# Shift and scale of the first two channel tiles: column products on TensorE instead of a running sum on VectorE

## Chip, cores and metric

The kernel runs on one core of a Trainium2 chip. The metric is the device time of one execution in microseconds (us); the median of several runs counts. Names of engines: PE is TensorE (PEld its weight loads), DVE is VectorE, ACT is ScalarE, POOL is GpSimd, SP is the engine whose queue issues most of the DMAs (transfers between HBM and on-chip memory).

## What is computed

One layer of a block with four parallel groups of attention heads, on 1024 latent tokens and 256 context tokens of width 2048, all in float32. What matters here is the start: the modulation of the normalised input by a vector that is made from the conditioning vector `c`.

```python
sh_x, sc_x, gt_x = jnp.split((jax.nn.silu(c) @ w_ada[l] + b_ada[l])[:, None, :], 3, axis=-1)
h_x = rms_norm(x, norm_g[l]) * (1 + sc_x) + sh_x
px = split_cols(h_x @ w_in[l])
```

So the shift `sh_x` and the scale `sc_x`, 2048 channels each, are a vector of 2048 entries times the first 4096 columns of the matrix `w_ada` (2048 rows). The attention, the output projection and the residual follow and are not touched by the change.

## The kernel before

**Tiles of channels.** The 2048 channels are 16 tiles of 128; on chip a channel is a partition. The first half of the latent tokens (512) is modulated and projected in five chunks of channel tiles, `chunks = [(0, 2), (2, 2), (4, 4), (8, 4), (12, 4)]` (first tile, number of tiles). The text calls them the first to the fifth chunk.

**Making a chunk** (`modulate`). First `ada_cols(k0, nk, 0, ax, shx)` makes shift and scale of the chunk: it loads `w_ada` in 16 blocks of 128 rows (tag `pt`, seven buffers of 4 KB per partition; in the first two chunks one buffer holds two row blocks, so eight buffers are filled by 16 loads of 256 KB). Each row block is multiplied by its entries of silu(c), one scalar per partition, and added to a sum `acc`: the first one or two blocks by ACT (L970), the others by DVE (L972, an operation of 512 elements per partition in the first two chunks and 1024 in the later ones). In the first two chunks there are two sums, for even and odd blocks, added at the end (L975). Then the partitions of the sum are added up by PE: for each channel tile one product with `acc` as the stationary operand and one column of ones as the moving operand (L979). DVE adds the bias and forms shift and scale (L982 to L984). Second, `h_build` transposes the normalised tokens by PE (L185), applies scale and shift by ACT (L187), and splits the result into a rounded part `b` (L188, ACT) and a rest (L189, DVE).

**Using a chunk** (`start`, `wide`, `three`). The projections of the chunk are products of 128x512 (L1099 to L1101, three for each tile and weight), 84 of them for a chunk of two tiles and 168 for a chunk of four. Their weights come by `w_piece`: a load on POOL's queue (L208) into `wr`, a rounded part `wh` by ACT (L220) and a rest `wl` by DVE (L221). A sum over chunks is kept in on-chip memory (L1135 by ACT in the first chunk, L1137 by DVE in the others).

**Ahead of the first chunk.** Four tiles of 128 tokens are loaded and normalised (`load_norm`: squares by ACT L151, small operations of DVE and ACT, L154 to L161, scaling by DVE, L163). Then 48 transposes (L1168) whose result nobody reads keep PE busy; they read the fourth of these tiles. Their PSUM tile and those of L979 and L185 share two buffers (`px`).

**What sets the order.** The code of two chunks is written interleaved (the second chunk is made while the first is used, and so on), and a scheduler then orders the instructions of each engine, under priorities; loads of `w_ada` are pinned to the order of the code on SP's queue. An engine works through its instructions strictly in that order.

Of the kernel before, what the change touches and what calls it, by code (L numbers as in the profile page):

```python
# [11 lines left out]
ALU = mybir.AluOpType  # L12
# [3 lines left out]
D = 2048  # L16
# [17 lines left out]
def hybrid_block(ctx, tc, x, c, cx, c_ctx, norm_g, w_ada, b_ada, w_in, w_out,  # L34
# [3 lines left out]
    pe, act, dve, pool, sp = nc.tensor, nc.scalar, nc.vector, nc.gpsimd, nc.sync  # L38
# [16 lines left out]
    def pin(i):  # L55
        return tc.keep_in_program_order(i) if strict[0] else i
# [5 lines left out]
    def T(shape, tag, dt=F32):  # L62
        uid[0] += 1
        return sb.tile(shape, dt, name=f"{tag}_{uid[0]}", tag=tag, bufs=BUFS[tag])

    def P(pool_, tag, bufs, n=512):
        uid[0] += 1
        return pool_.tile([128, n], F32, name=f"{tag}_{uid[0]}", tag=tag, bufs=bufs)
# [13 lines left out]
    def px():  # L82
        return P(ps, "x", 2)
# [5 lines left out]
    ident = cp.tile([128, 128], F32, name="ident")  # L89
# [76 lines left out]
    ax = cp.tile([128, 16], F32, name="ax")  # L166
    shx = cp.tile([128, 16], F32, name="shx")
# [13 lines left out]
    def h_build(k, xts, hT, a, sh, bank=None):  # L181
        hi, lo, n = hT
        tp = (bank or px)()
        for i in range(n // 128):
            pe.transpose(out=tp[:, 128 * i:128 * i + 128], in_=xts[i][k // 8][:, 128 * (k % 8):128 * (k % 8) + 128], identity=ident)  # L185
        ft = tmp()
        act.activation(ft[:, :n], tp[:, :n], AF.Identity, bias=sh[:, k:k + 1], scale=a[:, k:k + 1])  # L187
        act.copy(hi(k), ft[:, :n])  # L188
        dve.tensor_tensor(lo(k), ft[:, :n], hi(k).bitcast(F32), op=ALU.subtract)  # L189
# [760 lines left out]
    def ada_cols(k0, nk, vec, a_, s_):  # L950

        w, rb = 128 * nk, 4 // nk
        src = w_ada[0, :, 0:2 * D].rearrange("r (a n) -> r a n", a=2)
        na = min(rb, 2)
        acc = T([128, na, 2, w], "pt")
        for t in range(16 // rb):
            wt = T([128, rb, 2, w], "pt")
            for i in range(rb):
                k = rb * t + i
                if i == 0 or nk > 1:  # L960
                    ni = rb if nk == 1 else 1
                    if ni == 1:
                        pin(sp.dma_start(wt[:, i], src[128 * k:128 * k + 128, :, 128 * k0:128 * k0 + w]))
                    else:
                        for j in range(2):
                            pin(sp.dma_start(wt[:, :, j], src[128 * k:128 * k + 128 * rb, j, 128 * k0:128 * k0 + w]
                                             .rearrange("(r p) n -> p r n", p=128)))
                ak = acc[:, k % na]
                if k < na:
                    act.activation(ak, wt[:, i], AF.Copy, bias=0.0, scale=sil[:, vec, k:k + 1])  # L970
                else:
                    dve.scalar_tensor_tensor(ak, wt[:, i], sil[:, vec, k:k + 1], ak, op0=ALU.mult, op1=ALU.add)  # L972
            yield 0.25 * nk * rb
        if na == 2:
            dve.tensor_tensor(acc[:, 0], acc[:, 0], acc[:, 1], op=ALU.add)  # L975
        mp = px()
        for i in range(2):
            for j in range(nk):
                pe.matmul(mp[:, 4 * i + j:4 * i + j + 1], lhsT=acc[:, 0, i, 128 * j:128 * j + 128], rhs=ones[:, 0:1],  # L979
                          start=True, stop=True)  # L980
        ks = slice(k0, k0 + nk)
        dve.tensor_tensor(s_[:, ks], mp[:, 0:nk], bshc[:, ks], op=ALU.add)  # L982
        dve.tensor_tensor(a_[:, ks], mp[:, 4:4 + nk], bscc[:, ks], op=ALU.add)
        dve.scalar_tensor_tensor(a_[:, ks], a_[:, ks], 1.0, ngc[:, ks], op0=ALU.add, op1=ALU.mult)  # L984

    late = tc.keep_in_program_order

    grow_d = Dr([1, D], "grow")
# [62 lines left out]
    sil = cp.tile([128, 2, 16], F32, name="sil")  # L1051
# [5 lines left out]
    ngc, bshc, bscc, bgtc = cols[:, 2, :], cols[:, 3, :], cols[:, 4, :], cols[:, 5, :]  # L1057
# [88 lines left out]
    x0 = [load_norm(x[0, 128 * i:128 * i + 128, :], "kv") for i in range(4)]  # L1146

    def modulate(k0, nk):
        yield from ada_cols(k0, nk, 0, ax, shx)
        for k in range(k0, k0 + nk):  # L1150
            h_build(k, x0, hT0, ax, shx)

# [13 lines left out]
    for i in range(48):  # L1166
        j = 128 * (i % 4)
        pe.transpose(out=warm[:, j:j + 128], in_=x0[3][i // 4 % 2][:, j:j + 128], identity=ident)  # L1168
    run(modulate(*chunks[0]))
    gain = cp.tile([128, 16], F32, name="gain")  # L1170

# [23 lines left out]
    for n, (k0, nk) in enumerate(chunks):  # L1195
        if n == 4:
            load_gains()
        nxt = modulate(*chunks[n + 1]) if n + 1 < len(chunks) else iter(())
        interleave(enabled(k0 + nk), nxt, 8 * nk, 4.0 * (chunks[n + 1][1] if n + 1 < len(chunks) else 1))
# [139 lines left out]
```

## Time and profile before

| | |
|---|---|
| median of 3 runs | 2462.31 us (2461.33 to 2463.77) |
| profiled execution, its own time | 2464.92 us |
| its span in the trace | 2463.1 us |
| PE busy | 2366.9 us, 96% of the span, 12069 instructions |
| DVE busy | 1592.0 us, 65% |
| ACT busy | 1161.0 us, 47% |
| mean granted clock of PE | 0.993 of 2.4 GHz |
| memory read and written | 322.85 MB and 52.55 MB |

A row of a timeline tells the start, the length, engine, line, operation, what it writes and reads, how many instructions are merged into the row, and in brackets how long the engine had been idle before and what ended that. PE's products are pipelined: the length of one is longer than the distance to the next, so a price per instruction is read from a row that merges several. A row of a table of windows tells for a stretch the busy time of each engine with the number of instructions, the granted clock of PE, the busy share of the DMA engines and the GB/s they moved.

### The profile page before, as it was taken

Reading aid. Unit: us, or ns where it says so; the run is one execution under the profiler, and the core shown is the slowest. Engines: PE = TensorE matmul, PEld = TensorE weight load, DVE = VectorE, ACT = ScalarE, POOL = GpSimd, SP = SyncE. Lnnn points to the kernel's source line nnn. Section 1 sums busy time; section 2 is a strip of 40 time slices with the busy share of each in tenths; the row PEclk is TensorE's granted clock in tenths of the full one; section 3 lists DMA queues with packets and bytes.
Section 4 is the critical chain, followed back from the end, with each engine's and each line's share of the span. In section 5 each row is a group of like instructions: output and inputs, shape, how many; then the busy total and the mean of one; then the engine's idle time right before and its main releaser. Section 6 shows DMA issues by size and latency. Waiting matters only on the chain.

```text
span 2463.1 us, 34299 instructions
## 1 busy us (share of the span) xinstructions
PE 2366.9 (96%) x12069; PEld 1950.4 (79%) x12069; DVE 1592.0 (65%) x2875; ACT 1161.0 (47%) x2330; POOL 146.4 (6%) x159
## 2 busy tenths in 40 slices
PE   5999898999999999999999999999999999999999
PEld 4788675888888878777888878788888788887787
DVE  6986887754323277665677888866667776674433
ACT  4333553754322275344465665755556554443321
POOL 1121101000000010001000011100000000000000
PEclk9999999999999999999999999999999999999999
DMA  9996887933332356665343444643335443335633
GB/s 310 311 318 210 247 253 227 281 112 83 88 105 69 102 178 175 196 196 155 94 133 95 120 145 127 185 121 106 92 108 150 144 119 110 111 95 144 185 128 128
DMA packets 426485, 385.33 MB, mean 156 GB/s; under 512 B 78164, under 2 KB 323520, under 8 KB 426312
## 3 DMA queue, kind: packets, MB, share of 16 engines
q1 hardware_dynamic: 421672, 367.92, 49.6%
q0 software_dynamic: 4640, 15.21, 2.0%
q8 instruction: 95, 1.56, 0.3%
q14 instruction: 78, 0.64, 0.1%
HBM read 322.85 MB, written 52.55 MB: 152 GB/s over the span
## 4 chain that ended last, share of the span: by engine, by line
PE 69%; DVE 7%; DMA 4%; ACT 3%; issue 3%; POOL 0%; SPq 0%; DVEq 0%; POOLq 0%; ACTq 0%
PE acc L237 11%; PE acc L236 11%; PE acc L239 10%; PE x L788 3%; PE S_d L721 3%; PE o L809 2%; PE S_a L721 2%; PE o L810 2%; PE o L811 2%; PE a L417 2%; PE a L416 2%; PE a L415 2%; PE acc L415 1%; PE acc L416 1%; PE acc L417 1%
## 5 line engine op out<-in xcount | busy, mean ns | idle before, releaser
L220 ACT CAST wh<-wr 128x512 fp32r<-128x512 f32 x576 | 357.1, 621 | 758.1 <-PE acc L237 267.7
L221 DVE TENSOR_TENSOR wl<-wr,wh 128x512 fp32r<-128x512 f32 x576 | 405.2, 706 | 445.3 <-ACT wh L220 436.5
L236 PE MATMUL acc<-b,wh 128*128 128x512 f32 x1536 | 627.7, 409 | 13.6 <-ACT wh L220 6.9
L237 PE MATMUL acc<-b,wh 128*128 128x512 f32 x1536 | 621.2, 404 | 0.8 <-DVE b L604 0.8
L239 PE MATMUL acc<-b,wl 128*128 128x512 f32 x1504 | 608.7, 405 | 5.3 <-DVE wl L221 5.2
L236 PEld LDWEIGHTS acc<-b,wh 128*128 128x128 f32 x1536 | 291.2, 190 | 66.5 <-ACT wh L220 9.0
L237 PEld LDWEIGHTS acc<-b,wh 128*128 128x128 f32 x1536 | 291.6, 190 | 62.8 <-issue 1.3
L239 PEld LDWEIGHTS acc<-b,wl 128*128 128x128 f32 x1504 | 284.7, 189 | 70.2 <-DVE wl L221 9.6
L793 ACT CAST pt<-x 128x512 fp32r<-128x512 f32 (+3 forms) x312 | 144.2, 481 | 129.2 <-PE x L788 127.2
L788 PE MATMUL x<-ident,e 128*128 128x128 f32 x944 | 178.6, 273 | 6.9 <-DVE pt L794 2.5
L794 DVE TENSOR_TENSOR pt<-x,pt 128x512 fp32r<-128x512 f32 (+3 forms) x312 | 169.0, 555 | 9.6 <-ACT pt L793 8.4
L972 DVE SCALAR_TENSOR_TENSOR pt<-pt,sil,pt 128x1024 f32<-128x1024 f32 (+1 forms) x133 | 155.0, 1176 | 8.6 <-DMA pt<-in_w_ada_dram 8.0
L788 PEld LDWEIGHTS x<-ident,e 128*128 128x128 f32 x944 | 118.2, 140 | 33.2 <-DVE sm L733 5.9
L810 PE MATMUL o<-pt,kv 128*128 128x256 f32 (+1 forms) x496 | 140.8, 284 | 1.6 <-DVE sm L753 0.9
L809 PE MATMUL o<-pt,kv 128*128 128x256 f32 (+1 forms) x496 | 141.1, 284 | 0.6 <-ACT pt L793 0.5
L811 PE MATMUL o<-pt,kv 128*128 128x256 f32 (+1 forms) x496 | 138.9, 280 | 0.0
L721 PE MATMUL S_d<-kv,q 128*128 128x512 f32 (+1 forms) x480 | 118.0, 358 | 1.8 <-DVE q L604 1.4
L303 POOL TENSOR_TENSOR tmp<-tmp,mm 128x512 f32<-128x512 f32 x30 | 48.8, 1625 | 1112.3 <-DMA tmp<-tmp 246.4
L809 PEld LDWEIGHTS o<-pt,kv 128*128 128x128 f32 x496 | 93.5, 188 | 12.3 <-ACT pt L793 9.0
L721 PEld LDWEIGHTS S_d<-kv,q 128*128 128x128 f32 x480 | 85.2, 189 | 19.9 <-ACT e L734 2.5
L810 PEld LDWEIGHTS o<-pt,kv 128*128 128x128 f32 x496 | 93.5, 188 | 7.3 <-DVE pt L794 3.0
L811 PEld LDWEIGHTS o<-pt,kv 128*128 128x128 f32 x496 | 93.6, 189 | 2.2
(268 smaller groups left out, 4194.1 us busy)
## 6 DMA issues: line engine op xcount, KB each, us to landing
wr<-in_w_in_dram SPq DMA_DIRECT2D x326, 256.0 KB
pt<-in_w_ada_dram SPq DMA_DIRECT2D x144, 512.0 KB
wr<-in_w_out_dram SPq DMA_DIRECT2D x128, 256.0 KB
mm<-in_k_rope_dram SPq DMA_DIRECT2D x30, 512.0 KB
wr<-in_w_in_dram POOLq DMA_DIRECT2D x58, 256.0 KB, 5.8
wr<-in_w_in_dram SPq DMA_DIRECT2D x104, 128.0 KB
pt<-in_w_ada_dram SPq DMA_DIRECT2D x32, 256.0 KB
tmp<-in_x_dram SPq DMA_DIRECT2D x32, 256.0 KB
```

The lines of the kernel that those rows point to most:

```text
L220: act.copy(wh, wr)
L221: dve.tensor_tensor(wl, wr, wh.bitcast(F32), op=ALU.subtract)
L236: pe.matmul(acc[:, :n], lhsT=wh[:, j, :], rhs=hi(k), start=(k == 0), stop=False)
L237: pe.matmul(acc[:, :n], lhsT=wh[:, j, :], rhs=lo(k), start=False, stop=(end and wl is None))
L239: pe.matmul(acc[:, :n], lhsT=wl[:, j, :], rhs=hi(k), start=False, stop=end)
L721: pe.matmul(S_[:, o:o + n], lhsT=lt, rhs=rt_, start=(m == 0), stop=(m == len(terms) - 1))
L788: pe.transpose(out=tp[:, 128 * (n - g):128 * (n - g) + 128], in_=E[:, c0:c0 + 128], identity=ident)
L794: dve.tensor_tensor(dl, src, dh.bitcast(F32), op=ALU.subtract)
L809: pe.matmul(ov, lhsT=vh, rhs=ph, start=(m == 0), stop=False)
L810: pe.matmul(ov, lhsT=vh, rhs=pl, start=False, stop=False)
L811: pe.matmul(ov, lhsT=vl, rhs=ph, start=False, stop=(m == len(order) - 1))
L972: dve.scalar_tensor_tensor(ak, wt[:, i], sil[:, vec, k:k + 1], ak, op0=ALU.mult, op1=ALU.add)
```

## The change

A second generator, `ada_cols_pe`, makes the shift and scale of the first chunk; the other four chunks and the context tokens keep `ada_cols`. It has no sum on DVE or ACT: every row block of `w_ada`, as loaded, is the stationary operand of products whose moving operand is one column, the 128 entries of silu(c) that belong to the block's rows. There are 16 row blocks, two halves (shift and scale) and two channel tiles, hence 64 such products, accumulated in eight columns of one PSUM tile that a product with zeros opens. They are written in the order of the loads and kept in it. Lines behind the new function have numbers higher by 25 (L979 stays, L1099 becomes L1124, L1168 becomes L1193).

```diff
+    def ada_cols_pe(k0, nk, vec, a_, s_):
+        w, rb = 128 * nk, 4 // nk
+        src = w_ada[0, :, 0:2 * D].rearrange("r (a n) -> r a n", a=2)
+        mp = px()
+        zero = T([128, 8], "sm")
+        pool.memset(zero, 0.0)
+        pe.matmul(mp[:, 0:8], lhsT=ident, rhs=zero, start=True, stop=False)
+        for t in range(16 // rb):
+            wt = T([128, rb, 2, w], "pt")
+            for i in range(rb):
+                k = rb * t + i
+                pin(sp.dma_start(wt[:, i], src[128 * k:128 * k + 128, :, 128 * k0:128 * k0 + w]))
+                for j in range(2):
+                    for n in range(nk):
+                        tc.keep_in_program_order(
+                            pe.matmul(mp[:, 4 * j + n:4 * j + n + 1], lhsT=wt[:, i, j, 128 * n:128 * n + 128],
+                                      rhs=sil[:, vec, k:k + 1], start=False, stop=(k == 15 and j == 1 and n == nk - 1)))
+            yield 0.25 * nk * rb
+        ks = slice(k0, k0 + nk)
+        dve.tensor_tensor(s_[:, ks], mp[:, 0:nk], bshc[:, ks], op=ALU.add)
+        dve.tensor_tensor(a_[:, ks], mp[:, 4:4 + nk], bscc[:, ks], op=ALU.add)
+        dve.scalar_tensor_tensor(a_[:, ks], a_[:, ks], 1.0, ngc[:, ks], op0=ALU.add, op1=ALU.mult)
...
     def modulate(k0, nk):
-        yield from ada_cols(k0, nk, 0, ax, shx)
+        yield from (ada_cols if k0 else ada_cols_pe)(k0, nk, 0, ax, shx)
```

The scheduler's order moves with it, at the start of the program only. Names carry a running number; `x` are PSUM tiles, `kv` the normalised tokens.

PE, behind the 48 transposes, before: the four products of L979, then the eight transposes of `h_build`.

```order
L1168 MATMUL x_372<-ident,kv_349 128x128 x4
L979 MATMUL x_463<-ones_r,pt_421 128x1 x4
L185 MATMUL x_471<-ident,kv_276 128x128
L185 MATMUL x_471<-ident,kv_300 128x128
L185 MATMUL x_471<-ident,kv_324 128x128
L185 MATMUL x_471<-ident,kv_348 128x128
L185 MATMUL x_480<-ident,kv_276 128x128
```

PE, the same place with the change.

```order
L1193 MATMUL x_372<-ident,kv_349 128x128 x4
L994 MATMUL x_421<-sm_422,ident 128x8
L1003 MATMUL x_421<-sil,pt_425 128x1 x8
L1003 MATMUL x_421<-sil,pt_436 128x1 x8
L1003 MATMUL x_421<-sil,pt_447 128x1 x8
L1003 MATMUL x_421<-sil,pt_458 128x1 x8
L1003 MATMUL x_421<-sil,pt_469 128x1 x8
L1003 MATMUL x_421<-sil,pt_480 128x1 x8
L1003 MATMUL x_421<-sil,pt_491 128x1 x8
L185 MATMUL x_516<-ident,kv_276 128x128
```

Four transposes stand ahead of the last eight products, which read `pt_502`, and four behind them. The products of the first chunk's projections follow in both.

DVE, from the end of the first chunk's sum, before.

```order
L975 TENSOR_TENSOR pt_421<-pt_421 128x512
L982 TENSOR_TENSOR shx<-x_463,cols 128x2
L983 TENSOR_TENSOR ax<-x_463,cols 128x2
L984 SCALAR_TENSOR_TENSOR ax<-ax,cols 128x2
L972 SCALAR_TENSOR_TENSOR pt_512<-pt_527,sil,pt_512 128x512 x2
L972 SCALAR_TENSOR_TENSOR pt_512<-pt_547,sil,pt_512 128x512
L189 TENSOR_TENSOR b_252<-tmp_476,b_251 128x512
L189 TENSOR_TENSOR b_252<-tmp_485,b_251 128x512
L972 SCALAR_TENSOR_TENSOR pt_512<-pt_547,sil,pt_512 128x512
L972 SCALAR_TENSOR_TENSOR pt_512<-pt_568,sil,pt_512 128x512 x2
L221 TENSOR_TENSOR wl_535<-wr_532,wh_534 128x512
```

DVE with the change; the row ahead of the three small ones is the scaling of the last tokens.

```order
L163 TENSOR_SCALAR kv_349<-kv_349,st_361 128x1024
L1007 TENSOR_TENSOR shx<-x_421,cols 128x2
L1008 TENSOR_TENSOR ax<-x_421,cols 128x2
L1009 SCALAR_TENSOR_TENSOR ax<-ax,cols 128x2
L189 TENSOR_TENSOR b_252<-tmp_521,b_251 128x512
L189 TENSOR_TENSOR b_252<-tmp_530,b_251 128x512
L972 SCALAR_TENSOR_TENSOR pt_557<-pt_572,sil,pt_557 128x512
L221 TENSOR_TENSOR wl_580<-wr_577,wh_579 128x512
L972 SCALAR_TENSOR_TENSOR pt_557<-pt_572,sil,pt_557 128x512
L972 SCALAR_TENSOR_TENSOR pt_557<-pt_592,sil,pt_557 128x512 x2
```

Before, the second chunk's sum (`pt_512`) begins ahead of L189, with three operations, and has six behind it when the first `wl` of L221 stands in the order. With the change the sum (`pt_557`) begins behind L189 and has one.

ACT, behind the last small operations of the normalisation, before.

```order
L156 ACTIVATE st_361<-st_361 128x1
L970 ACTIVATE pt_512<-pt_513,sil 128x512 x2
L187 ACTIVATE tmp_476<-x_471,shx,ax 128x512
L187 ACTIVATE tmp_485<-x_480,shx,ax 128x512
L188 CAST b_251<-tmp_476 128x512
```

ACT with the change.

```order
L156 ACTIVATE st_361<-st_361 128x1
L187 ACTIVATE tmp_521<-x_516,shx,ax 128x512
L187 ACTIVATE tmp_530<-x_525,shx,ax 128x512
L188 CAST b_251<-tmp_521 128x512
L188 CAST b_251<-tmp_530 128x512
L970 ACTIVATE pt_557<-pt_558,sil 128x512 x2
```

The two operations that open the second chunk's sum moved from ahead of the first chunk's L187 to behind its L188. From the third chunk on the orders of all engines are equal, but for the line numbers.

## Rows read from the trace of the kernel before

**Rows 1.** The page, part 1: busy time, share, instructions of PE.

```profile
PE 2366.9 (96%) x12069; PEld 1950.4 (79%) x12069; DVE 1592.0 (65%) x2875; ACT 1161.0 (47%) x2330; POOL 146.4 (6%) x159
```

**Rows 2.** Windows, four stretches: window, PE, PEld, DVE, ACT, POOL, clock, DMA, GB/s.

```profile
20.00:30.00 10.00, 1.15 (x6) 1.15 (x7) 8.55 (x24) 4.47 (x14) 0.00 (x0) 1.00 1.07 345
...
60.00:80.00 20.00, 17.34 (x81) 13.54 (x82) 18.73 (x25) 6.74 (x12) 3.62 (x6) 1.00 1.02 375
...
200.00:250.00 50.00, 50.00 (x216) 40.23 (x215) 32.19 (x43) 20.82 (x35) 4.05 (x4) 1.00 0.68 209
```

**Rows 3.** Timeline of DVE, 19 to 30 us.

```profile
19.94 0.15 DVE L154 TENSOR_REDUCE st<-st 128x1 f32<-128x4 f32 x1
...
22.32 1.42 DVE L163 TENSOR_SCALAR kv<-kv,st 128x1024 f32<-128x1024 f32 x2
23.65 0.75 DVE L972 SCALAR_TENSOR_TENSOR pt<-pt,sil,pt 128x512 f32<-128x512 f32 x1
...
27.39 0.75 DVE L972 SCALAR_TENSOR_TENSOR pt<-pt,sil,pt 128x512 f32<-128x512 f32 x1
28.05 1.41 DVE L163 TENSOR_SCALAR kv<-kv,st 128x1024 f32<-128x1024 f32 x2
```

**Rows 4.** Timeline of PE, 26 to 48 us.

```profile
28.85 8.21 PE L1168 MATMUL x<-ident,kv 128*128 128x128 f32 x48 [23.41 <-DVE kv L163]
36.90 0.95 PE L979 MATMUL x<-ones_r,pt 128*128 128x1 f32 x8
37.71 1.18 PE L185 MATMUL x<-ident,kv 128*128 128x128 f32 x8
40.72 1.56 PE L1099 MATMUL a<-b,wh 128*128 128x512 f32 x4 [1.83 <-ACT b L188]
```

**Rows 5.** Timeline of PE, 380 to 395 us.

```profile
380.65 0.39 PE L236 MATMUL acc<-b,wh 128*128 128x512 f32 x1
380.88 0.40 PE L237 MATMUL acc<-b,wh 128*128 128x512 f32 x1
...
386.86 1.95 PE L979 MATMUL x<-ones_r,pt 128*128 128x1 f32 x16
```

**Rows 6.** Timeline of ACT, 33 to 48 us.

```profile
33.58 1.39 ACT L970 ACTIVATE pt<-pt,sil 128x512 f32<-128x512 f32 x2 [8.55 <-DMA pt<-in_w_ada_dram]
38.72 1.45 ACT L187 ACTIVATE tmp<-x,shx,ax 128x512 f32<-128x512 f32 x2 [3.75 <-PE x L185]
40.06 1.13 ACT L188 CAST b<-tmp 128x512 fp32r<-128x512 f32 x2
```

**Rows 7.** Timeline of DVE, 33 to 62 us, and one row at 88 us.

```profile
34.80 0.69 DVE L975 TENSOR_TENSOR pt<-pt 128x512 f32<-128x512 f32 x1
...
38.24 2.08 DVE L972 SCALAR_TENSOR_TENSOR pt<-pt,sil,pt 128x512 f32<-128x512 f32 x3
40.70 1.29 DVE L189 TENSOR_TENSOR b<-tmp,b 128x512 fp32r<-128x512 f32 x2 [0.39 <-ACT b L188]
41.91 2.07 DVE L972 SCALAR_TENSOR_TENSOR pt<-pt,sil,pt 128x512 f32<-128x512 f32 x3
46.25 0.69 DVE L221 TENSOR_TENSOR wl<-wr,wh 128x512 fp32r<-128x512 f32 x1 [2.27 <-ACT wh L220]
...
62.13 0.15 DVE L984 SCALAR_TENSOR_TENSOR ax<-ax,cols 128x2 f32<-128x2 f32 x1
...
88.54 0.16 DVE L982 TENSOR_TENSOR shx<-x,cols 128x4 f32<-128x4 f32 x1 [1.10 <-PE x L979]
```

**Rows 8.** Windows of 2 us: the transposes at first, later, and the first projections.

```profile
30.00:32.00 2.00, 2.00 (x11) 2.00 (x10) 2.00 (x4) 0.00 (x0) 0.00 (x0) 1.00 1.09 347
...
34.00:36.00 2.00, 2.00 (x18) 2.00 (x17) 1.45 (x3) 0.97 (x2) 0.00 (x0) 1.00 1.09 349
...
42.00:44.00 2.00, 2.00 (x6) 1.55 (x5) 1.99 (x3) 0.00 (x0) 0.00 (x0) 0.50 1.02 316
```

**Rows 9.** Timeline of PE, 55 to 75 us.

```profile
66.11 1.19 PE L1099 MATMUL a<-b,wh 128*128 128x512 f32 x4 [2.33 <-ACT b L188]
```

## Prediction

> **What bounds the kernel now.** First the page: PE is busy for 2366.9 of 2463.1 us [rows 1]. What is left is 96 us, so almost any microsecond that PE starts later or works longer is a microsecond of the kernel, unless a gap of PE swallows it. Second the windows: from 20 to 30 us PE does 1.15 us of work and DVE 8.55; from 60 to 80 us DVE is busy for 18.73 of 20 us and PE has gaps, 17.34 of 20; from 200 to 250 us PE has none, and DVE is at 32.19 of 50 [rows 2]. So the start belongs to DVE, and later PE alone decides. Third the timelines of the first 62 us, where the change is.
>
> The path to the first projection is to be seen there. DVE scales the last tokens at 28.05 [rows 3], PE's block of 48 transposes starts when that operation has written its first half, at 28.85, and takes 8.21 us; L979 follows without a gap and ends at 37.85; the first projection (L1099) starts at 40.72 [rows 4]. The sum of the first chunk on DVE ended at 35.49 (L975) [rows 7], while PE was still in its block. The removed sum is thus not itself what PE waited for. What it did to the path is to stand between the operations of the last normalisation.
>
> **The change, part by part.**
>
> *Removed from DVE and ACT.* Fourteen sums of 128x512 (three in 2.07 us, 0.67 each [rows 7]), one addition of 0.6, two ACT operations (0.66 each, half of the row of two [rows 6]): 10 us of DVE. Only this counts: six of the sums stand between 23.65 and the second scaling at 28.05 [rows 3]. Without them the chain from L154 to L163 begins at 23.65. For the tile before it took 2.4 us (19.94 to 22.32 [rows 3]), with squares of ACT in between that are gone by then. So the scaling starts between 24.5 and 26.05; I take 25.15, a chain of 1.5 us, since two short ACT steps and six small DVE steps remain and nothing else is queued. That is 2.9 us earlier. The block of transposes then runs from 25.95 to 34.0 (8.05 us to the next product, as before).
>
> *Added on PE.* One product with zeros and 64 with one column. The price is L979's, which has the same shapes. Here the counts matter: in the order L979 stands with four products for a chunk of two tiles, and in the trace the same place shows eight [rows 4]; sixteen stand for eight [rows 5]. A float32 product is two instructions of PE. Sixteen take 1.95 us, of which 0.25 is the length of the last, so 0.113 us each [rows 5]; the eight at 36.90 give 0.10 [rows 4]. So 130 instructions by 0.113 are 14.7 us (13.0 at the lower price). They stand between the block and the first projection with nothing beside them that PE could do: the order has four transposes there (4 x 0.11, from eighteen in 2 us [rows 8]) and no projection. The end is 34.0 + 14.7 + 0.45 + 0.15 = 49.3 instead of 37.85: **11.4 us later**. The product with zeros is in the count, and its memset on POOL lies in the first microseconds, where POOL is idle; no cost.
>
> The Trainium skill, "FP8 and Floating Point Precision", section TensorE Precision Notes, counts four passes through the array for true float32. The trace shows two instructions [rows 4, 5]; at four of that price the sum would be 14.7 us more, and the measured row decides, since it holds whatever passes there are.
>
> *From there to the first projection*: before, 37.85 to 40.72, 2.9 us through shift and scale, two operations of L187 and one of L188 [rows 4, 6]. All of it stays, L187 now waits for the small DVE operations alone. No change.
>
> *Moved: the second chunk's sum.* Before, ACT opened it at 33.58 [rows 6], DVE did three operations at 38.24 and three at 41.91, both ahead of the first L221, which waited until 46.25 for a buffer that PE's first projections free [rows 7]. With the change ACT opens it behind L188, and DVE has only one operation ahead of that L221. DVE, idle for some 22 us while PE works through the columns, can use none of it, as it works strictly in order and L1007 waits for PE. So relative to the first projection the second chunk's sum has three operations more to do (2.0 us), and two of those that had filled the wait for L221 come behind it (1.4 us). Some of that returns: L984 came at 62.13, behind an operation of the third chunk's sum [rows 7], and now follows its neighbours. I take **3 us**, between 0 and 3.4. It counts as long as DVE sets the pace, which it does until the third chunk's shift and scale at 88.54, as DVE has hardly an idle microsecond from 60 to 80 [rows 2, 7]. PE's gap of 2.33 us at 66.11 [rows 9] may close on the way, but then PE waits longer at the third chunk.
>
> *Loads.* As many, of the same size, in the same order on SP's queue. Without the sum's own buffer seven buffers take the first seven pairs of loads; the eighth waits for PE's first eight products, 1.8 us after 34.0. At 347 GB/s [rows 8] its 0.5 MB take 1.5 us, and PE needs it some 11 us after that. The second chunk's loads follow at the pace of PE's products, one pair in 1.8 us, and are there before DVE asks for them at 52. Cover for all of it is the column phase; without it the eighth pair alone would cost some 2 to 4 us. No cost.
>
> *Later.* From the third chunk on the orders are equal, so every engine runs the same program later by the same amount. Loads wait for buffers, not for the hour, so they move too.
>
> The sum: +11.4 + 3.0 = +14.4, on the profiled execution's 2464.92 gives 2479.3. That execution is 2.6 above the median of the runs, so on the median's footing **2476.7 us**.
>
> **Rivals.**
>
> *The clock falls in the column phase.* In the block, eleven transposes in 2 us become eighteen [rows 8], that is PE passed from the lower level (1.2 GHz) to the upper (2.4), though the clock column says 1.00 in both. After the eight products, eight transposes and 1.83 us of idling the projections ran at the lower level, 0.50 from 42 to 44 us [rows 4, 8]. Whether one-column products keep the upper level, no row shows for more than 1.95 us. At the transposes' ratio (18 to 11) all 130 would cost 9.4 us more; the block's start leaves perhaps half of them at full rate, so some 5 us, and 1.7 for a later rise under the projections: 2483.5. Chance 0.27.
>
> *Only the start counts.* The shift of DVE's work is swallowed: PE's gap of 2.33 us closes [rows 9], and the sums of the third chunk catch up. +11.4 - 2.3 = +9.1: 2471.4. Chance 0.13.
>
> *Not slower: the column costs next to nothing.* Among projections of 512 columns the distance is 0.233 us with the weight load wholly hidden [rows 5]; if a weight load hid under the product before it here too, an instruction with one column would cost its column alone, 0 at the lower end. Then the end of the columns is 34.6, 3.25 us earlier than 37.85, and with DVE's 3 us the whole is -0.25: 2462.1. It decides below 0.04 us an instruction, where 130 of them stay under 5.2 us. Against it speak both rows of L979, at two and a half times that. The Trainium skill, "TensorE: Matmul & The Clock Gate", section Back-to-back issue gap, gives about 60 cycles, 25 ns, for 1 to 64 columns; by that the phase would last an estimated 3.3 us and the time be 2465.1. L979's rows disagree, 0.10 to 0.113. Chance 0.04.
>
> *The price is not L979's*: more passes or a wait for each accumulation into the same column, up to twice: 2491. Chance 0.03.
>
> **How the numbers follow.** The forecast itself has 0.53. The likeliest time is 2476.7. Its own spread: 1.7 less at the lower price, 1.1 less or 0.9 more for the start of the block, up to 1.5 either way for where the clock changes. The range takes in the rival below and most of the falling clock: 2471 to 2486. A measurement of this kernel can tell 0.2% (4.9 us) from no change. Faster by more: 0.02. Within: 0.03. Slower: 0.95.
>
> **What would show it.** The block of transposes starts near 26; 128 instructions of L1003 in some 14.5 us with PE busy and DVE idle throughout; the first L1124 near 52; the first L972 behind L189; L982 of the third chunk near 103 instead of 88.54; PE equally busy from 200 us on. Wrong would be: L1003 denser than 0.1 us or beyond 0.17, PE waiting for a load there, or a delay that shrinks behind 100 us.

## The result and the profile after

The changed kernel takes 2494.86 us (median of four runs, 2489.74 to 2498.87), the kernel before beside it 2463.04 (four runs, 2461.33 to 2464.13): a ratio of 1.0128, 95% interval 1.0112 to 1.0143. That is 31.8 us slower, where 14.4 were forecast, and outside the range. The sign and the place were right; one price was not.

The profiled execution after took 2489.74 us (span 2488.0), the lowest of the four. All steps below are followed in it, against 2464.92 (span 2463.1) before: 24.8 us. The page of the profile, part 1, beside [rows 1]:

```profile
PE 2392.2 (96%) x12191; PEld 1973.4 (79%) x12191; DVE 1586.1 (64%) x2860; ACT 1160.2 (47%) x2328; POOL 144.7 (6%) x160
```

PE is busy for 25.3 us more, and the kernel is 24.8 us longer. PE idles about as much as before. The profile calls PE equally busy, 96%, in both kernels, so the slower work in between does not show there. The timeline of PE after, where before [rows 4] stands (start, duration, engine, line, operation, count, idle time before):

```profile
25.98 7.33 PE L1193 MATMUL x<-ident,kv 128*128 128x128 f32 x48 [20.34 <-DVE kv L163]
33.15 0.29 PE L994 MATMUL x<-sm,ident 128*128 128x8 f32 x2
33.29 20.95 PE L1003 MATMUL x<-sil,pt 128*128 128x1 f32 x112
54.10 1.09 PE L185 MATMUL x<-ident,kv 128*128 128x128 f32 x4
54.99 3.41 PE L1003 MATMUL x<-sil,pt 128*128 128x1 f32 x16
58.81 1.09 PE L185 MATMUL x<-ident,kv 128*128 128x128 f32 x4 [0.41 <-DVE ax L1008]
61.28 2.07 PE L1124 MATMUL a<-b,wh 128*128 128x512 f32 x4 [1.38 <-ACT b L188]
```

The block starts 2.87 us earlier, as forecast. The 128 instructions of L1003 then run to 58.4 and never wait for a load, but take 24 us in place of 14.5, and the first projection is at 61.28, 20.6 us later than before. The forecast had 11.4. Windows of 2 us of the same kernel for PE (busy time, instructions, granted clock, DMA share, GB/s) show where:

```profile
34.00:36.00 2.00, 2.00 (x20) 1.00 0.03 8
36.00:38.00 2.00, 2.00 (x14) 0.67 0.78 246
38.00:40.00 2.00, 2.00 (x11) 0.50 0.80 259
...
64.00:66.00 2.00, 2.00 (x6) 0.50 0.82 261
66.00:68.00 2.00, 2.00 (x7) 0.65 0.04 10
68.00:70.00 2.00, 2.00 (x11) 1.00 0.49 51
```

PE is busy for 2.00 of 2 us in each of them. The granted clock falls to 0.50, the lower level of 1.2 GHz, at about 36.7 us, in the midst of the column products, and comes back at about 67, under the projections. Instructions fall from 20 to 11 in a window. (A window also counts an instruction that began before it, so its count gives a price that is too low; a long row is safer: 16 in 3.41 us from 54.99 on, and 24 in 5.12 in e3_noblock below, 0.213 each, against 0.10 at the upper level.)

The timeline of DVE after, beside [rows 7]:

```profile
58.44 0.16 DVE L1007 TENSOR_TENSOR shx<-x,cols 128x2 f32<-128x2 f32 x1 [31.85 <-PE x L1003]
61.26 1.29 DVE L189 TENSOR_TENSOR b<-tmp,b 128x512 fp32r<-128x512 f32 x2 [2.40 <-ACT b L188]
62.47 0.75 DVE L972 SCALAR_TENSOR_TENSOR pt<-pt,sil,pt 128x512 f32<-128x512 f32 x1
67.02 0.69 DVE L221 TENSOR_TENSOR wl<-wr,wh 128x512 fp32r<-128x512 f32 x1 [3.81 <-ACT wh L220]
...
81.88 0.16 DVE L982 TENSOR_TENSOR shx<-x,cols 128x2 f32<-128x2 f32 x1 [1.60 <-PE x L979]
...
113.33 0.16 DVE L982 TENSOR_TENSOR shx<-x,cols 128x4 f32<-128x4 f32 x1 [1.11 <-PE x L979]
```

DVE waits 31.85 us for the columns with nothing ahead in its queue that it could do, then starts the second chunk's sum behind L189, as forecast. The third chunk's shift is at 113.33 instead of 88.54: +24.8. From that row to the end of the span there are 2374.7 us, and before 2374.6. So everything that the change costs in the profiled execution has been paid by 113 us.

### The profile page after: what moved, and what is told of

Read it like the earlier page. It is cut to its first block, busy times and chain, and to the rows that moved or that the text cites. A ratio compares the mean times of both kernels' runs of the same rounds, so it can differ in the third digit from the quotient of the medians.

```text
span 2488.0 us, 34520 instructions
## 1 busy us (share of the span) xinstructions
PE 2392.2 (96%) x12191; PEld 1973.4 (79%) x12191; DVE 1586.1 (64%) x2860; ACT 1160.2 (47%) x2328; POOL 144.7 (6%) x160
## 4 chain that ended last, share of the span: by engine, by line
PE 75%; DVE 9%; DMA 7%; issue 4%; ACT 3%; SPq 1%; POOL 0%; DVEq 0%; ACTq 0%; POOLq 0%
PE acc L236 11%; PE acc L237 11%; PE acc L239 11%; PE x L788 3%; PE S_d L721 3%; DMA pt<-in_w_ada_dram 2%; PE S_a L721 2%; PE o L809 2%; PE o L810 2%; PE o L811 2%; PE a L417 2%; PE a L416 2%; PE a L415 2%; PE acc L416 1%; PE acc L415 1%
## 5 line engine op out<-in xcount | busy, mean ns | idle before, releaser
L221 DVE TENSOR_TENSOR wl<-wr,wh 128x512 fp32r<-128x512 f32 x576 | 402.8, 701 | 443.1 <-ACT wh L220 432.6
L972 DVE SCALAR_TENSOR_TENSOR pt<-pt,sil,pt 128x1024 f32<-128x1024 f32 (+1 forms) x119 | 145.0, 1225 | 5.7 <-DMA pt<-in_w_ada_dram 5.1
```

What stands on the lines that cost most here:

```text
L221: dve.tensor_tensor(wl, wr, wh.bitcast(F32), op=ALU.subtract)
```

## The experiments

Theory A: the granted clock falls during the column products, and about 97 of the 130 instructions cost twice the price that I took. Rival B: the time is lost behind the start, in DVE's order. Rival C: the number of instructions, or the weight load in front of each, sets the price, whatever the clock (the expectation of e1_fill8 calls a form of this theory B).

The table gathers the eleven runs. "Sums ahead" counts how many of the second chunk's 14 sums (L972) stand on DVE ahead of the first chunk's L189; "third chunk" is L982 (e4_order: L983) for four tiles; times in us of the profiled execution, but for the median. Each experiment has its ratio to the kernel before as timed beside it on the same chip (median 2464.79 for e1 to e4, 2465.13 for e5 to e8, 2463.94 for e9 and e10).

| kernel | median | ratio [95%] | first projection | third chunk | sums ahead |
|---|---|---|---|---|---|
| before | 2463.04 | 1 | 40.72 | 88.54 | 3 |
| changed kernel | 2494.86 | 1.0128 [1.0112, 1.0143] | 61.28 | 113.33 | 0 |
| e1_fill8 | 2484.11 | 1.0091 [1.007, 1.0112] | 63.64 | 100.58 | 12 |
| e2_half | 2479.56 | 1.0065 [1.0043, 1.0086] | 49.61 | 102.92 | 0 |
| e3_noblock | 2482.50 | 1.0080 [1.0062, 1.0098] | 50.58 | 102.63 | 0 |
| e4_order | 2486.16 | 1.0093 [1.0074, 1.0113] | 74.05 | 108.31 | 14 |
| e5_after | 2494.75 | 1.0119 [1.0102, 1.0135] | 61.66 | 114.97 | 0 |
| e6_fill4 | 2494.11 | 1.0118 [1.0099, 1.0137] | 70.31 | 117.36 | 6 |
| e7_row | 2475.75 | 1.0041 [1.0027, 1.0055] | 53.12 | 91.93 | 11 |
| e8_row_noblock | 2461.75 | 0.9990 [0.9977, 1.0003] | 40.77 | 85.80 | 7 |
| e9_wide32 | 2484.40 | 1.0081 [1.0066, 1.0096] | 58.87 | 108.24 | 1 |
| e9_wide128 | 2473.12 | 1.0038 [1.0024, 1.0051] | 52.02 | 92.90 | 10 |
| e10_row_gap | 2460.16 | 0.9980 [0.9968, 0.9992] | 40.92 | 83.96 | 7 |

### Eight unread transposes behind each row block

```diff
+                for f_ in range(8):
+                    j = 128 * (f_ % 3) + 128
+                    tc.keep_in_program_order(
+                        pe.transpose(out=warm[:, j:j + 128], in_=x0[3][f_ % 2][:, j:j + 128], identity=ident))
```

> Behind each of the 16 row blocks of the column phase stand eight transposes of 128x128 whose result nobody reads (128 in all, written to the tile of the block of transposes). Theory A (the column products are dear because PE falls to the lower level, 0.50, 3.4 us into the phase, and one-column products do not raise it): the transposes hold the granted clock at 1.00, the 128 instructions of the column products take about 0.10 us each, 13 us, the transposes 0.11 each, 14 us; the phase lasts some 27 us, no longer than the 25.2 us without them by more than 2, though PE does twice as many instructions, and the first projections run at 0.233 us. Time 2489 to 2495. Theory B (0.18 us is the price of an accumulating product with a fresh stationary operand, whatever the clock): the clock column says 1.00, but the column products keep 0.18 and the phase lasts 23 + 14 = 37 us; time 2505 or more.

Its PE timeline, the third and the last row block (L1003 the columns, L1008 the fillers), and the first projection:

```profile
36.64 0.95 PE L1003 MATMUL x<-sil,pt 128*128 128x1 f32 x8
37.45 1.07 PE L1008 MATMUL x<-ident,kv 128*128 128x128 f32 x8
...
59.00 0.95 PE L1003 MATMUL x<-sil,pt 128*128 128x1 f32 x8
59.81 1.07 PE L1008 MATMUL x<-ident,kv 128*128 128x128 f32 x8
...
63.64 1.19 PE L1128 MATMUL a<-b,wh 128*128 128x512 f32 x4 [1.61 <-ACT b L188]
```

and a window late in the phase (entries as in [rows 2]):

```profile
56.00:60.00 4.00, 4.00 (x39) 4.00 (x39) 0.01 (x1) 0.00 (x0) 0.00 (x0) 1.00 0.88 265
```

The price of the columns stays at 0.81 us for eight from first to last (36.64 to 37.45, 59.00 to 59.81), 0.10 an instruction, and the clock's row says 1.00 up to the projections. So with 128 unread transposes more the phase ends only 2.4 us later, and the median is 10.75 us below that of the changed kernel (2484.11 against 2494.86), less than the 2489 to 2495 expected. By the ratios it is 9 us, and 7 against the repeat of the changed kernel below, whose interval overlaps with this one; the profiled execution here, 2491.44, is the slowest of its four. That the price is 0.10 at 1.00 is therefore firmer than the size of the gain. The column products as such cost what I had taken; the rest came with the lower level. But the edit also moved DVE's order: 12 sums run ahead of L189 here, none in the changed kernel. What of the gain comes from that, this run cannot tell.

The Trainium skill, "TensorE: Matmul & The Clock Gate", section Part 4: PE-mode transpose, says that the full clock does not engage for transposes. The traces differ, and they decide: in the block of 48, where PE does nothing else, eleven transposes in 2 us become eighteen [rows 8], and with transposes between them the columns ran at 1.00 for 27 us, where without them the clock fell to 0.50.

### Half of the products

This kernel leaves out the products of the odd row blocks but the last, so that 36 of 64 remain.

```diff
-                    for n in range(nk):
+                    for n in range(nk if k % 2 == 0 or k == 15 else 0):
```

> Leaves out the column products of the odd row blocks but the last, so 36 instead of 64 (the shift and scale of the first two channel tiles lack those rows); all loads stay. Theory A: 56 instructions at the lower level are gone, 56 x 0.182 = 10.2 us, and the fall of the clock stays at the same place; the first projection starts near 51 instead of 61.3 us and the time is 10 us below the change's 2494.9, 2485. If the phase were bound by the loads instead, which are all still there, the first projection would stay near 61 and the time near 2495.

```profile
33.15 9.42 PE L1003 MATMUL x<-sil,pt 128*128 128x1 f32 x56
...
43.32 3.41 PE L1003 MATMUL x<-sil,pt 128*128 128x1 f32 x16
```

Those are rows of its PE timeline. 56 instructions fewer brought the first projection forward by 11.7 us, 0.21 each, where 0.113 would give 6.3. The marginal instruction costs the lower level's price, as theory A has it. The median fell by 15.3 us and the profiled execution by 12.3; no sum stands ahead of L189, as in the changed kernel.

### Without the block of transposes

```diff
-    warm = px()
-    for i in range(48):
-        j = 128 * (i % 4)
-        pe.transpose(out=warm[:, j:j + 128], in_=x0[3][i // 4 % 2][:, j:j + 128], identity=ident)
```

> The block of 48 transposes is left out; the column products can start when their rows have landed, some 21 us, instead of 33.3. Theory A: they run at the lower level throughout, 130 x 0.182 = 23.7 us, end near 46, first projection near 49 instead of 61.3, 12 us less; the projections still start at the lower level. Time 2483. If the block had been worth its time by what it gives the column phase (31 instructions at the upper level, 2.5 us) and to later clock, the gain would be half of that or less, 2489 or more.

```profile
20.19 5.12 PE L1003 MATMUL x<-sil,pt 128*128 128x1 f32 x24
...
30.64 17.07 PE L1003 MATMUL x<-sil,pt 128*128 128x1 f32 x80
```

As expected: the first projection at 50.58, the median 2482.50. PE did not pass to the upper level in this phase: 5.12/24 and 17.07/80 are both 0.213 us, for 27 us on end, with PE busy throughout. The block, whose purpose is to raise the clock, delays the columns by 13 us, and what it gained was lost at 36.7: leaving it out is worth some 12 us in the median.

### The second chunk's sum pinned ahead

```diff
-                    dve.scalar_tensor_tensor(ak, wt[:, i], sil[:, vec, k:k + 1], ak, op0=ALU.mult, op1=ALU.add)
+                    pin_(dve.scalar_tensor_tensor(ak, wt[:, i], sil[:, vec, k:k + 1], ak, op0=ALU.mult, op1=ALU.add))
...
-    run(modulate(*chunks[0]))
+    first = ada_cols_pe(*chunks[0], 0, ax, shx)
+    for _ in range(9):
+        next(first)
+    second = modulate(*chunks[1])
+    for _ in range(8):
+        next(second)
+    run(first)
```

> The second chunk's sum on DVE and ACT is recorded and pinned ahead of the first chunk's shift and scale, so that DVE works on it while PE does the column products. Of the 24.8 us by which the third chunk's shift and scale came later in the change, 20.6 stand at the first projection already. If the rest (4.2 us) is DVE's sum that was put behind L189, the time falls by 4 to 8 us below 2494.9 (PE then has no gap between the first three chunks): 2488. If PE was the bound there anyway, or the pinned sums, whose loads wait for PE's products, hold up the first chunk's shift and scale instead, nothing is gained: 2495.

Its DVE timeline:

```profile
46.79 1.41 DVE L973 SCALAR_TENSOR_TENSOR pt<-pt,sil,pt 128x512 f32<-128x512 f32 x2 [20.36 <-DMA pt<-in_w_ada_dram]
...
67.53 0.15 DVE L1009 TENSOR_TENSOR shx<-x,cols 128x2 f32<-128x2 f32 x1
...
72.72 0.16 DVE L983 TENSOR_TENSOR shx<-x,cols 128x2 f32<-128x2 f32 x1 [4.30 <-PE x L980]
...
108.31 0.16 DVE L983 TENSOR_TENSOR shx<-x,cols 128x4 f32<-128x4 f32 x1 [0.51 <-PE x L980]
```

A mixed result, and a rival came true beside the theory: the pinned sums (L973 here) wait for their loads, which wait for buffers that the slow columns free (from 20 to 70 us SP's queue waited 16.8 us for L1004, the column products, ahead of loads of L963), so the first chunk's shift comes at 67.53, 9 us later than in the changed kernel. In spite of a first projection that is 12.8 us later, the third chunk is 5 us earlier, and the median is 8.7 us lower (the profiled execution, 2489.54, is the slowest of its four and only 0.2 us shorter than that of the changed kernel). So the place of these sums seems to matter by more than the 3 us that I had put on it; but the edit has a cost of its own and does not measure it.

### The changed kernel again, and four transposes for eight

```diff
-                for f_ in range(8):
+                for f_ in range(4):
```

(against e1_fill8). e5_after is the changed kernel itself.

> The changed kernel once more, beside the next three on the same chip, so that they can be compared with it and not only with the kernel before. Theory A (TensorE's granted clock falls during the column products, after which everything waits on them at 0.18 us an instruction in place of 0.10): 2490 to 2499 us again, some 30 us over the kernel before. Its rival (the earlier 2494.86 was an unlucky chip and my 14.4 us were right): 2477 to 2482.

> Four unread transposes behind each of the 16 row blocks, where e1_fill8 had eight. In e1_fill8 a row block with its eight products and eight transposes took 27.8/16 = 1.74 us at the upper clock, of which 0.95 were the products' eight instructions, so a transpose costs about 0.10. Theory A, if four are enough to hold the clock: phase of 16 x (0.95 + 0.4) = 21.6 us, its end near 55, first product of the projections near 57.5, third chunk's L986 (the sums behind the three chunks) near 97 to 105, time 2476 to 2484. If four are too few: the clock falls on the way, 0.182 an instruction from there, phase of 30 us or more, end at 63 or later, time 2492 to 2503. Rival B (the order of VectorE's work was what helped e1_fill8, and the fillers only added to the delay): VectorE's order here stands nearer to that of the changed kernel, so the time stays at 2490 or more although the clock holds.

The repeat gave 2494.75, 29.6 over the kernel before: the result stands. (The 0.18 us of an expectation was counted from windows; by long rows the lower level's price is 0.213.) In e6_fill4 the PE timeline reads

```profile
40.87 0.95 PE L1003 MATMUL x<-sil,pt 128*128 128x1 f32 x8
41.69 0.69 PE L1008 MATMUL x<-ident,kv 128*128 128x128 f32 x4
42.16 1.71 PE L1003 MATMUL x<-sil,pt 128*128 128x1 f32 x8
...
70.31 2.07 PE L1128 MATMUL a<-b,wh 128*128 128x512 f32 x4 [1.37 <-ACT b L188]
```

and its window of 42 to 44 us

```profile
42.00:44.00 2.00, 2.00 (x13) 0.54 0.08 27
```

With four the clock fell all the same, at 42.1, later than in the changed kernel but still early in the phase, and the eight columns went from 0.95 to 1.71 us. Now 64 fillers are in the way as well, and the first projection is 8.65 us later than in e5_after, on the same chip. The median is the same within its runs, 2494.11 (2490.46 to 2497.97). Of the 8.65 us 6.3 were won back by the third chunk, and that separates the two mechanisms: of its sums six stand ahead of L189, none in e5_after, and from first projection to third chunk it takes 47.1 us instead of 53.3. Both are needed to explain the times: A for the phase, B for what follows it.

### The operands' places changed

```diff
+                    pe.matmul(rp[0:1, :], lhsT=sil[:, vec, k:k + 1], rhs=wt[:, i].rearrange("p a n -> p (a n)"),
+                              start=(k == 0), stop=(k == 15)))
...
+        row = tmp()
+        act.copy(row[0:1, :], rp[0:1, :])
+        mp = px()
+        for j in range(2):
+            for n in range(nk):
+                pe.matmul(mp[:, 4 * j + n:4 * j + n + 1], lhsT=row[0:1, w * j + 128 * n:w * j + 128 * n + 128],
+                          rhs=ones[0:1, 0:1], start=True, stop=True)
```

> The same sums with the operands' places changed: the column of sil is the stationary operand (one column) and the 512 elements of a row block move, so that each of the 16 products is 2 instructions of 512 columns in place of 16 instructions (8 products) of one column; then one copy of the row by ScalarE and 4 products that turn it into columns. The block of 48 transposes stays. A 512-column instruction takes 0.233 us at the upper clock and 0.43 at the lower one in the changed kernel. Theory A (a clock that falls for want of moving columns): the clock stays at 1.00, phase of 32 x 0.233 = 7.5 us if an instruction runs like those of the projections and 16 us if these fp32 passes take twice as long; end between 41 and 50, first projection between 45 and 54, time 2468 to 2479, so 15 us or more below the changed kernel. Rival C (the phase is long because of the weight load of 128 x 128 elements in fp32 in front of each product, whatever the clock): here the loads are of one column, so the phase is as short, but the clock would have to fall here too. What tells them apart is the clock's row in the phase.

> As e7_row, without the 48 unread transposes, so that the products start when the first rows of w_ada land, near 20 us, in place of 33. Theory A: the clock starts at its lower level (e3_noblock: 0.21 us an instruction throughout, one column each) but rises a few us into a phase that moves 512 columns at a time; 32 instructions of 0.43 to 0.86 at first, then 0.23 to 0.43: end between 32 and 44, first projection between 36 and 48 (kernel before: 40.72), time 2455 to 2472. If moving columns do not raise the clock: 32 x 0.86 = 27.5 us, end near 48, first projection near 52 at the lower clock, time 2475 to 2484, about that of e3_noblock.

Rows of the PE timeline of e7_row, a window in the phase, and one behind it, in the gaps ahead of the projections:

```profile
33.45 13.89 PE L1021 MATMUL x<-pt,sil 128*1 128x512 f32 x32
...
53.12 2.07 PE L1149 MATMUL a<-b,wh 128*128 128x512 f32 x4 [1.60 <-ACT b L188]
```

```profile
44.00:46.00 2.00, 2.00 (x6) 1.00 0.87 258
...
50.00:52.00 2.00, 1.08 (x4) 0.51 1.09 363
```

and of e8_row_noblock, with two windows of the phase:

```profile
19.77 16.09 PE L1021 MATMUL x<-pt,sil 128*1 128x512 f32 x32 [14.28 <-DMA pt<-in_w_ada_dram]
...
40.77 1.66 PE L1149 MATMUL a<-b,wh 128*128 128x512 f32 x4 [2.06 <-ACT b L188]
```

```profile
22.00:24.00 2.00, 2.00 (x4) 1.00 1.11 363
...
26.00:28.00 2.00, 2.00 (x6) 1.00 1.10 350
```

In e7_row the clock stays at 1.00 through the phase, where rival C had it fall; 32 instructions take 13.89 us, 0.434 each. That is near the slow end of the expectation. Without the block the products reach the upper level by themselves: the first six start some 0.85 us apart, those from 24.5 us on 0.43 (32 instructions in 16.09 us, where twice 0.434 for each would make 27.8), and the first projection is at 40.77, where the kernel before has it, at 40.72. The median is 2461.75, 0.999 of before: the first projection comes no later for it, and DVE is busy for 9 us less (1583.0 against 1592.0). It is no gain that can be told from none.

A float32 product of 512 columns is two instructions of 0.434, and one of the projections', which read operands in the shorter format fp32r [rows 7], takes 0.233 in the same trace: 3.7 to 1. The Trainium skill, "FP8 and Floating Point Precision", section TensorE Precision Notes, says four passes for true float32; 3.7 comes near that. At one column it did not show: there an instruction takes 0.10 us, and with 128 columns (e9_wide128 below) 0.113, so the columns are not what these 0.10 us are spent on.

### The column of silu(c) repeated

```diff
-                            pe.matmul(mp[:, 4 * j + n:4 * j + n + 1], lhsT=wt[:, i, j, 128 * n:128 * n + 128],
-                                      rhs=sil[:, vec, k:k + 1], start=False,
+                            pe.matmul(mp[:, 128 * (2 * j + n):128 * (2 * j + n) + 128], lhsT=wt[:, i, j, 128 * n:128 * n + 128],
+                                      rhs=sil[:, vec, k:k + 1].to_broadcast([128, 128]), start=False,
```

(e9_wide32 with 32 for the width.)

> The changed kernel's column products with the column of sil repeated 32 times as the moving operand, so that each of the same 128 instructions moves 32 columns in place of one (the sums come out the same, 32 times over, and the first of each 32 is read). Same loads, same weights, same order. If the clock falls for want of moving columns and 32 are enough: it stays at 1.00, 128 instructions at 0.10 to 0.12 = 13 to 15 us from 34.5, end near 49, first product of the projections near 52 (changed kernel 61.3 to 61.7), time 2474 to 2482. If 32 are too few: the clock falls later than in the changed kernel (there 3.4 us into the phase), and the time lies between 2482 and 2496. If the columns do not matter (what counts is the number of instructions or of weight loads): it falls at the same place, 2490 to 2499.

> The same with 128 repeated columns. A transpose's instruction moves 128 columns of 128 rows in 0.10 us at the upper clock in the block ahead of the phase, so 128 instructions should take 13 to 16 us. Theory A: the clock stays at 1.00, end between 48 and 51, first product of the projections between 51 and 54, time 2474 to 2484: a phase with 128 times the columns, and shorter by 9 us. Rival (weight loads or instructions set the clock): it falls, and the time is 2490 or more.

Rows of the PE timeline of e9_wide32, and its window of the fall:

```profile
33.51 20.62 PE L1003 MATMUL x<-sil,pt 128*128 128x32 f32 x120
...
58.87 2.07 PE L1124 MATMUL a<-b,wh 128*128 128x512 f32 x4 [1.37 <-ACT b L188]
```

```profile
38.00:40.00 2.00, 2.00 (x16) 0.76 0.93 284
```

and of e9_wide128, with a window late in the phase and the first of DVE's sums in it:

```profile
33.09 14.45 PE L1003 MATMUL x<-sil,pt 128*128 128x128 f32 x128
...
52.02 1.80 PE L1124 MATMUL a<-b,wh 128*128 128x512 f32 x4 [2.06 <-ACT b L188]
```

```profile
44.00:46.00 2.00, 2.00 (x20) 1.00 1.00 321
```

```profile
43.39 1.42 DVE L972 SCALAR_TENSOR_TENSOR pt<-pt,sil,pt 128x512 f32<-128x512 f32 x2 [17.26 <-DMA pt<-in_w_ada_dram]
```

This is the cleanest pair. Weights, their loads and the number of instructions are those of the changed kernel (only the product with zeros is wider), and rival C falls with it as the cause of the extra time: with 128 times as many columns the 128 instructions take 14.45 us, 0.113 each, less than the 24 us with one column, and the clock stays at 1.00. With 32 columns it still fell, at about 39.0. The first projection is 9.3 us earlier with 128, the median 21.7 lower (by the ratios 1.0128 and 1.0038 it is 22). The 9.3 are the clock, but for 0.2 us by which the columns begin earlier here. The other half goes with DVE's order, which the scheduler changed along with the edit: 10 sums ahead of L189, from 43.39 on, while PE works at the columns. Only e4_order changes that order with nothing else, and it has a cost of its own, so the share of the order is read from the table and not measured by itself.

### The idle gap filled

```diff
+    warm = px()
+    for i in range(16):
+        j = 128 * (i % 4)
+        tc.keep_in_program_order(
+            pe.transpose(out=warm[:, j:j + 128], in_=x0[3][i // 4 % 2][:, j:j + 128], identity=ident))
```

behind e8_row_noblock's first chunk.

> e8_row_noblock with 16 unread transposes in front of the first product of the projections, where TensorE stood idle for 2.06 us for ScalarE's hi parts and then ran the first eight products 0.43 apart at the lower clock, to 44.7. The fillers fill 1.4 to 1.7 us of that gap. Theory A: the clock stays at 1.00, the first products come 0.233 apart, 2 us less, first product still at 40.8, time 2457 to 2461. If the gap does not cause the fall: no change, 2460 to 2464; if the fillers run behind the end of the wait: up to 1 us more.

```profile
39.19 1.97 PE L1221 MATMUL x<-ident,kv 128*128 128x128 f32 x16 [0.88 <-ACT tmp L187]
40.92 0.48 PE L1149 MATMUL a<-b,wh 128*128 128x512 f32 x1
41.23 0.39 PE L1150 MATMUL a<-b,wh 128*128 128x512 f32 x1
41.46 0.40 PE L1151 MATMUL a<-b,wl 128*128 128x512 f32 x1
```

```profile
40.00:42.00 2.00, 2.00 (x16) 1.00 1.10 348
```

The projections now come 0.23 us apart from the second on, at clock 1.00, where e8_row_noblock and the kernel before [rows 8] had 0.50 at 42 to 44 us. So the fall there came with the gap. The span is 2.3 us shorter than that of e8_row_noblock, 2 were expected. The median of 2460.16 is 0.998 of before, interval 0.9968 to 0.9992: the one version here whose interval lies below the kernel before, by about 4 us. From e8_row_noblock, with 0.9977 to 1.0003, it is not told apart by these runs.

## Why the prediction was wrong in size

Point by point, by its own steps:

- **The start of the block**, 25.95 forecast: 25.98. Right, and so was its reason, DVE's sums out of the last normalisation: the last scaling (L163) starts at 25.17, forecast 25.15.
- **The price of the columns**, 130 instructions by 0.113 = 14.7 us: this is the step that failed. L979's rows were measured at the upper level and last 1.95 us at most, and the change makes a phase of 24 us. At the upper level the price holds (0.10 in e1_fill8). In the changed kernel about 33 instructions ran at it, up to 36.7, and some 97 at the lower level, at 0.213. 97 x (0.213 - 0.113) = 9.7 us, and the first projection came 9.2 us later than the sum had it.
- **The falling clock** stood there as a rival with 0.27 and 2483.5, so the sum itself put it at nothing. Its mechanism was the true one, and it was undersized twice: the ratio of the levels was taken from counts in windows (18 to 11, 1.64), which count straddling instructions, and is 2.1 by durations; and "perhaps half" of the instructions at full rate was a guess, where it was a quarter. With the measured figures it gives 9.7 us more than the forecast, before DVE.
- **DVE's second sum**, 3 us: 4.2 in the profiled execution (52.05 us from first projection to third chunk, 47.82 before). Right in kind: DVE is busy for 1.5 us more in that stretch (43.74 against 42.23), waits 3.81 us ahead of the first L221 where it waited 2.27 [rows 7], and then 1.60 for PE at 81.88. What the later return of the clock, at 67, adds to it was not separated. The table shows how the stretch goes with the sums: with none ahead of L189 it takes 52.1 to 53.3 us in four runs, with 1 it is 49.4, with 3 47.8, with 6 47.1, with 7 45.0 and 43.0, with 10 to 12 40.9 to 36.9, with 14 34.3. That is about 1.2 us for a sum that itself takes 0.67, and other work moved with the sums. The 32 us in which DVE stands idle were an opportunity, and I only counted the loss against before. Some of it is given back after the third chunk: the span ends 2374.7 us behind that row in the changed kernel, 2382.8 in e7_row and 2389.1 in e1_fill8. Of this, 4.6 and 3.8 us are lost by the fourth chunk already (its L982 at 155.99, 139.20 and 147.02); the rest was not followed.
- **Loads**, no cost: L1003 never waits for one. Right.
- **Later**, a rigid shift: 2374.7 against 2374.6 us, 2374.8 in the repeat. Right for this change; the experiments with another order of DVE do not all keep it.
- **Below the known price** (the rival that the column costs next to nothing): excluded. 0.10 is the lowest price that any kernel here shows at one column with 128x128 weights. (By its own terms the estimate from 25 ns would be 2465.4, not 2465.1.)
- **The price is not L979's** (0.03, up to twice, 2491): that number comes near the measured one, but by luck, as its mechanism is not the one. With the same accumulation into the same columns an instruction takes 0.10 us in e1_fill8 at 1.00.
- **Only the start counts** (0.13): not so. The stretch from first projection to third chunk grew by 4.2 us, where this rival had it shrink by 2.3.

With the clock's 9.7 and DVE's 4.2 the sum is 11.4 + 9.7 + 4.2 = 25.3, on 2464.92 gives 2490.2; the profiled execution took 2489.74. That the two agree within 0.5 us is partly luck: the column phase began 0.85 us earlier than in the sum (33.15 against 34.0). The median lies 5 us above that. The longer runs show a lower mean clock (0.985 to 0.986 against 0.989). The second profile of the changed kernel (e5_after, 2491.63, clock 0.986) shows the same steps, with a fall at about 39 us, and one place where such time can be lost: from 2300 to 2310 and from 2320 to 2330 us it was granted 0.72 and 0.83, the first profile 1.00 in both, and the same instructions of DVE that start 1.5 us earlier than in the first profile near 2235 us start 1.9 us later near 2443. Whether the longer runs lose their 5 us there stays open.

## What to carry to other kernels

A price taken from a short group holds for the clock that this group ran at. Before multiplying it by a hundred, ask what the clock will do meanwhile, and price the phase at both levels in full: here a phase of one-column products counted as 100% busy, and its clock fell to 0.50 all the same. Where a sum over partitions must be done by TensorE, try it with the wide operand moving and the vector stationary; here 16 such products began at the lower level, reached the upper one without a block ahead of them, and left the first projection where it had been (40.77 against 40.72). And when an engine is made to wait for 30 us, look at what stands ahead of that wait in its queue: here it went with up to 15 us at the third chunk, of which part was given back later.

## What the runs showed that was not expected

- More work was faster: 128 added transposes (e1_fill8) took some 7 to 11 us off the median, and 128 times the moving columns (e9_wide128) some 22.
- One instruction with a fresh weight load costs about the same at the upper level with one column of float32 as with 128: 0.10 (e1_fill8) and 0.113 us (e9_wide128).
- The clock in the profile's rows can read 1.00 where PE works at the lower level: e3_noblock's columns take 0.213 us from 20 us on, the price that goes with 0.50 elsewhere, and the windows there say 1.00. The distance of equal instructions is the surer reading.
